# A four-layer hybrid trunk on one core: VectorE in traced order at the layer norms, six slots for split weights, the mixers' residual scaled at out_proj

## The chip, the cores and the metric

The kernel is one program on one core of a Trainium2 chip. The metric is device time in microseconds (us) of that core. The kernel before took 2769.28 us, the median of three runs between 2768.69 and 2770.76. The engines are TensorE (PE; its weight loads are PEld), VectorE (DVE), ScalarE (ACT), GpSimd (POOL) and SyncE (SP), which issues most of the transfers. An engine takes its instructions strictly in the order in which the program lists them, and an instruction whose input is not there holds up all that stand behind it on that engine.

## The reference

The kernel computes a decoder trunk of four layers on one sequence of 512 tokens with 1024 channels, all in float32. The mixers are Gated DeltaNet (GDN), HGRN2, GLA and GDN again. Each is followed by a dense SwiGLU channel mixer, and each of the eight branches ends in a residual and a layer norm:

```python
for i in range(DEPTH):                       # DEPTH = 4
    m = (gated_deltanet, hgrn2, gla)[i % 3](x, ...)      # each ends in  o @ w_out
    x = layer_norm(DN_ALPHA * x + m, mix_ln_g[i], mix_ln_b[i])
    x = layer_norm(DN_ALPHA * x + swiglu(x, ffn_w_in[i], ffn_w_down[i]), ffn_ln_g[i], ffn_ln_b[i])
return x

def layer_norm(x, g, b):
    mu = mean(x, -1); var = mean(square(x - mu), -1)
    return (x - mu) * rsqrt(var + LN_EPS) * g + b

def swiglu(x, w_in, w_down):
    gate, up = split(x @ w_in, 2)
    return (silu(gate) * up) @ w_down
```

## The kernel before

**Products.** Every float32 product is three matmuls: each operand is split into a high and a low part, and high by low, high by high and low by high are summed (mm3, L176 to L178). The activations live transposed in SBUF as xTh and xTl, with channels on the partitions and tokens along the rows. A weight block of 1 MB or less is loaded by SP, ACT copies it to a rounded high part (whi, L142), and DVE subtracts to get the low part (wlo, L144). These pairs live in the pool "wsplit", which has four slots for high and four for low parts. A fifth pair waits until PE has used the first for the last time.

**The norms.** out_proj and the FFN's second product end in down_norm. The 512 tokens are four tiles of 128. The last half of the output channels is done tile by tile from eight blocks of resident weights, called res, some of which stand in wsplit slots: down(i) on PE, 24 matmuls, then norm(i). norm(i) adds the residual (add_x, L331), takes the statistics (bn_stats L361, bn_aggr L364), works out the inverse root by ten instructions on one column (L365 to L377), and then ACT normalises the tile in two halves of 512 channels (L382; for the last tile's first half DVE does it, L380). PE then transposes the tile (tr(i): put_xT, L214, eight transposes into two PSUM tiles xtp). For each half the four 128-channel pieces get the norm's scale and bias on their way out of PSUM: pieces 0 and 2 by ACT (L224), 1 and 3 by DVE (L222), all into one tile xt. Then ACT copies the half to xTh (L226) and DVE subtracts to get xTl (L227).

**The order around a norm.** The next phase's first four weight slices, w0 to w3, are fed in between: begin() multiplies them with token columns 0 to 255 (tiles 0 and 1) first, and 256 to 511 afterwards. The traced order on PE is down(0), down(1), down(2) with tr(0) inside, down(3) with tr(1) inside, w0, tr(2), w1, tr(3), w2, w3, and then the other columns. Before GLA and GDN, w0 is a narrow slice of 16 matmuls (L190). manual_schedule holds PE to this order. The other engines get theirs from the framework's scheduler, which places each instruction by its estimate of when it can run. There are seven such norms, after four mixers and three FFNs. The last FFN writes the output and has no next phase.

**The residual.** x itself, needed again one branch later, also gets scale and bias, on POOL: affine(), two instructions per half tile (L390, L394), 16 in all, held back by a dependency until the last x^T is written. After an FFN's norm each half tile is then stored to DRAM (store, L385), and the next mixer loads it again in get_x (L236), when out_proj begins.

**The starts of the next mixers.** After an FFN's norm HGRN begins with forget gates and products on DVE (L1011, L1012, L901 to L917), GLA with a gate on ACT and DVE (L1074 to L1088), and GDN with a chain of small gate columns on DVE (gcols, L573 to L588), which PE needs at L590. At the mixers' end, finish() works out an inverse root over the heads (occ and rsq, L511 to L516, L133 to L137), DVE and POOL scale the heads by it (on, L519), and PE transposes them (ytp, L528) for out_proj.

Of the kernel before, what the change touches and what calls it, by code (L numbers as in the profile page):

```python
# [13 lines left out]
ALU = mybir.AluOpType  # L14
# [3 lines left out]
P = 128  # L18
T = 512
D = 1024  # L20
NT = T // P
# [16 lines left out]
class Net:  # L38
    def __init__(self, ctx, tc, a, out):
        self.tc, self.nc, self.a, self.out = tc, tc.nc, a, out  # L40
        pool = lambda name, bufs, **kw: ctx.enter_context(tc.tile_pool(name=name, bufs=bufs, **kw))
        self.cp = pool("const", 1)
        self.raw = pool("raw", 2)
        self.wsp = pool("wsplit", 4)
        self.xp = pool("xT", 1)
        self.ar = pool("arena", 1)
        self.col = pool("cols", 2)
        self.mid = pool("mid", 1)
        self.dr = pool("dram", 2, space=bass.MemoryType.DRAM)
        self.acc = pool("acc", 4, space=PSUM)  # L50
        self.mx = pool("mx", 4, space=PSUM)
        self.n = 0
        self.deferred, self.late, self.lmask = [], [], None
        self.lo_eng = self.nc.vector
        self.xT = tuple(self.xp.tile([P, KD, T], F32R, name=n) for n in ("xTh", "xTl"))
        self.consts()
# [172 lines left out]

    def get_x(self):  # L230

        x = []
        for i in range(NT):
            x.append([self.t2("st", s="x") for _ in range(2)])
            for e in range(2):
                self.nc.sync.dma_start(x[i][e], self.x_dram[i * P:(i + 1) * P, e * 512:(e + 1) * 512])  # L236
        return x

    def early(self, unit):
# [94 lines left out]
    def down_norm(self, kt, w, k0, pools, alpha, g, b, to_dram, to_out, rtags):  # L334

        nc, V = self.nc, self.nc.vector
        n = len(kt)
        lnw = []
        for v in (g, b):
            for e in range(2):  # L340
                t = self.t2("vz", s="lnw")
                nc.gpsimd.dma_start(t, v[e * 512:(e + 1) * 512].partition_broadcast(P))
                lnw.append(t)
        if not to_out:
            gb = self.columns(self.rows([v.rearrange("(k p) -> k p", p=P) for v in (g, b)]), "lngb")
        stats = self.small([P, NT, 2, 6], s="bnst")
        self.down_part(kt, w, k0, 0, pools[0], alpha)
        for i in range(NT):
            V.bn_stats(stats[:, i, 0], self.x[i][0])
        ps = [self.bank(pools[1], [P, 512], "dn") for _ in range(NT)]  # L350
        kr = n - self.NRES
        for k, wt in self.kblocks(w, 1, k0, k0 + kr):
            for i in range(NT):
                self.mm_tok(ps[i], i, kt[k - k0], wt, k == k0, False)
        res = list(self.kblocks(w, 1, k0 + kr, k0 + n, rtags))
        next(self.nxt)
        if to_dram:
            self.x_dram = self.dr.tile([T, D], F32, tag="xd", name=self.nm("xd"))

        def norm(i):  # L360
            V.bn_stats(stats[:, i, 1], self.add_x(ps[i], i, 1, alpha))  # L361
            c = self.small([P, 6], s="lnc", bufs=4)
            mean, var, vh, rstd, z, shift = (c[:, k:k + 1] for k in range(6))
            V.bn_aggr(c[:, 0:2], stats[:, i])  # L364
            V.tensor_scalar(vh, var, LN_EPS, -0.5, ALU.add, ALU.mult)  # L365
            V.tensor_scalar(rstd.bitcast(I32), vh.bitcast(I32), -0.5, RSQRT_MAGIC - float(0x40400000), ALU.mult, ALU.add)
            for _ in range(3):
                V.scalar_tensor_tensor(z, rstd, vh, rstd, ALU.mult, ALU.mult)
                V.scalar_tensor_tensor(rstd, z, 1.5, rstd, ALU.add, ALU.mult)
            x = self.x[i]  # L370
            if to_out:
                for e in range(2):
                    V.scalar_tensor_tensor(x[e], x[e], mean, lnw[e], ALU.subtract, ALU.mult)
                    V.scalar_tensor_tensor(x[e], x[e], rstd, lnw[2 + e], ALU.mult, ALU.add)
                    store(i, e, self.out[0])
                return
            V.scalar_tensor_tensor(shift, mean, -1.0, rstd, ALU.mult, ALU.mult)  # L377
            for e in range(2):
                if i == NT - 1 and e == 0:
                    V.tensor_scalar(x[e], x[e], mean, rstd, ALU.subtract, ALU.mult)  # L380
                else:
                    nc.scalar.activation(x[e], x[e], AF.Identity, bias=shift, scale=rstd)  # L382

        def store(i, e, dst):
            nc.sync.dma_start(dst[i * P:(i + 1) * P, e * 512:(e + 1) * 512], self.x[i][e])  # L385

        def affine(i):
            for e in range(2):
                r = self.x[i][e]
                first = nc.gpsimd.tensor_tensor(r, r, lnw[e], ALU.mult)  # L390
                if i == 0:
                    self.tc.add_manual_dep(first.ins, self.xT_done.name, mybir.DependencyInfo(
                        mybir.DependencyClass.Sync, mybir.DependencyReason.DATA), reason="x^T first")
                nc.gpsimd.tensor_tensor(r, r, lnw[2 + e], ALU.add)  # L394
                if to_dram:
                    store(i, e, self.x_dram)

        def down(i, k1, k2):
            for k, wt in res[k1:k2]:
                self.mm_tok(ps[i], i, kt[k - k0], wt, k == k0, k == k0 + n - 1)  # L400

        def tr(i):
            for e in range(2):
                self.put_xT(i, self.x[i][e], e, gb)

        with self.tc.manual_schedule(engines={mybir.EngineType.PE}):
            for i in range(NT):
                cut = 0 if to_out or i < 2 else i - 1
                down(i, 0, cut)
                if cut:  # L410
                    tr(i - 2)
                down(i, cut, None)
                norm(i)
            if not to_out:
                next(self.nxt)
                tr(2)
                next(self.nxt)
                tr(3)
                next(self.nxt)
        if not to_out:  # L420
            with self.tc.manual_schedule(engines={mybir.EngineType.Pool}):
                for i in range(NT):
                    affine(i)
# [358 lines left out]
    def solve(self, nt):  # L782

        nc = self.nc
        V, S, G, mm = nc.vector, nc.scalar, nc.gpsimd, nc.tensor.matmul
# [19 lines left out]
            V.tensor_tensor(pr[:, :, :c, :c], u8[:, :, :c, :c], m8[:, :, c:c + 1, :c].broadcast_to([P, 2, c, c]), ALU.mult)  # L805
            V.tensor_reduce(u8[:, :, :c, c], pr[:, :, :c, :c], AX.X, ALU.add)
        pr = sv((P, 8, 8, 8), "pr8")
        z = self.small([P, 8, 8], s="z8", bufs=1)
        V.tensor_tensor(pr, U[:, 0:8, None, 0:8].broadcast_to([P, 8, 8, 8]),
                        M[:, None, 8:16, 0:8].broadcast_to([P, 8, 8, 8]), ALU.mult)  # L810
        V.tensor_reduce(z, pr, AX.X, ALU.add)
# [375 lines left out]
```

## Time and profile before

| what | value |
|---|---|
| median of three runs | 2769.28 us |
| the profiled execution's own time | 2768.41 us |
| its span, first to last instruction | 2766.5 us |
| mean granted TensorE clock, of full speed | 0.986 |
| PE / PEld busy | 97% / 81% |
| DVE / ACT / POOL busy | 55% / 38% / 11% |

The profiled execution lies within the three runs. About 1.9 us of its time lie outside the span. PE's busy share is an upper bound, since the ends of pipelined matmuls are modelled; what is certain are the stretches in which PE did nothing, and the profile names for each the instruction that ended it. The granted clock is 1.0 at 2.4 GHz and 0.5 at 1.2 GHz.

### The profile page before, as it was taken

The page shows a single profiled execution, that of the slowest core. Times are in us where ns is not written, and L with a number is a line of the kernel's source. Part 1 is how long each engine was busy: PE and PEld are TensorE (multiplying, and loading weights), DVE is VectorE, ACT ScalarE, POOL GpSimd, SP SyncE. Part 2 cuts the span into 40 slices and gives each one's busy share as a digit, 9 for nine tenths or more (in the row PEclk, how much of TensorE's full clock was granted, in tenths as well). Part 3 has the DMA queues.
Part 4 walks back from the last instruction along what each step waited for, and adds up shares of the span by engine and source line. Part 5 has one row for each costly group of instructions (what it writes and reads, how often), then busy time and mean ns, then how long its engine had stood idle before and what let it go on. Part 6 is the DMA issues. An engine that isn't in the chain of part 4 may idle for free.

```text
span 2766.5 us, 37874 instructions
## 1 busy us (share of the span) xinstructions
PE 2672.5 (97%) x15279; PEld 2235.3 (81%) x15279; DVE 1512.6 (55%) x3015; ACT 1061.0 (38%) x2107; POOL 304.2 (11%) x316
## 2 busy tenths in 40 slices
PE   9999999999899999999999999999979999999998
PEld 8787888888777778888887888888877787888886
DVE  6667753333777776323366665333378576733335
ACT  5464542222444444222244644222235455422221
POOL 1111040001300004000030004000031111210000
PEclk9999999999999999999999999999989999999999
DMA  4213233233221232232322232232322132232222
GB/s 140 62 47 100 85 95 104 92 98 115 74 77 50 85 115 92 92 107 92 108 75 81 77 122 92 93 105 91 110 74 77 47 100 77 69 117 96 92 99 69
DMA packets 198719, 248.29 MB, mean 90 GB/s; under 512 B 8890, under 2 KB 152384, under 8 KB 198544
## 3 DMA queue, kind: packets, MB, share of 16 engines
q1 hardware_dynamic: 195152, 237.29, 26.8%
q0 software_dynamic: 3392, 8.59, 1.0%
q8 instruction: 120, 1.97, 0.3%
q14 instruction: 55, 0.45, 0.1%
HBM read 237.47 MB, written 8.39 MB: 89 GB/s over the span
## 4 chain that ended last, share of the span: by engine, by line
PE 82%; DVE 12%; issue 2%; ACT 2%; POOL 0%; DMA 0%; SPq 0%; DVEq 0%; ACTq 0%; POOLq 0%
PE pj L177 16%; PE pj L178 16%; PE pj L176 16%; PE dn L176 8%; PE dn L178 8%; PE dn L177 7%; DVE wlo L144 2%; DVE am L898 2%; DVE qk L616 1%; PE sc L931 1%; PE tp L491 1%; PE vp L177 1%; PE xtp L214 1%; PE vp L176 1%; PE kk L672 1%
## 5 line engine op out<-in xcount | busy, mean ns | idle before, releaser
L176 PE MATMUL pj<-xTl,whi 128*128 128x512 f32 (+1 forms) x2472 | 927.3, 375 | 0.0
L177 PE MATMUL pj<-xTh,whi 128*128 128x512 f32 (+1 forms) x2472 | 926.3, 375 | 0.0
L178 PE MATMUL pj<-xTh,wlo 128*128 128x512 f32 (+1 forms) x2472 | 925.4, 374 | 0.0
L144 DVE TENSOR_TENSOR wlo<-wraw,whi 128x1024 fp32r<-128x1024 f32 x400 | 509.9, 1277 | 688.7 <-ACT whi L142 682.9
L142 ACT CAST whi<-wraw 128x1024 fp32r<-128x1024 f32 x400 | 419.8, 1051 | 1160.6 <-PE pj L177 656.3
L177 PEld LDWEIGHTS pj<-xTh,whi 128*128 128x128 f32 x2472 | 470.8, 190 | 78.0 <-issue 0.7
L176 PEld LDWEIGHTS pj<-xTl,whi 128*128 128x128 f32 x2472 | 470.7, 190 | 78.0 <-issue 0.7
L178 PEld LDWEIGHTS pj<-xTh,wlo 128*128 128x128 f32 x2472 | 470.6, 190 | 77.8 <-issue 0.5
L440 DVE TENSOR_TENSOR sg<-sg,pj 128x512 f32<-128x512 f32 x88 | 60.4, 686 | 240.2 <-PE pj L178 240.2
L176 PE MATMUL dn<-wlo,hhi 128*128 128x512 f32 x416 | 161.8, 389 | 0.0
L177 PE MATMUL dn<-whi,hhi 128*128 128x512 f32 x416 | 161.8, 389 | 0.0
L178 PE MATMUL dn<-whi,hlo 128*128 128x512 f32 x416 | 161.8, 389 | 0.0
L390 POOL TENSOR_TENSOR x<-x,lnw 128x512 f32<-128x512 f32 x56 | 83.5, 1491 | 312.1 <-issue 243.9
L331 DVE SCALAR_TENSOR_TENSOR x<-x,dn 128x512 f32<-128x512 f32 x96 | 64.9, 685 | 61.2 <-PE dn L178 61.0
L394 POOL TENSOR_TENSOR x<-x,lnw 128x512 f32<-128x512 f32 x56 | 90.9, 1623 | 4.2
L177 PEld LDWEIGHTS dn<-whi,hhi 128*128 128x128 f32 x416 | 78.1, 188 | 16.3
L178 PEld LDWEIGHTS dn<-whi,hlo 128*128 128x128 f32 x416 | 78.1, 188 | 16.2
L176 PEld LDWEIGHTS dn<-wlo,hhi 128*128 128x128 f32 x416 | 78.1, 188 | 16.2
L176 PE MATMUL dn<-wlo,nt 128*128 128x512 f32 x224 | 87.5, 390 | 0.0
L178 PE MATMUL dn<-whi,nt 128*128 128x512 f32 x224 | 87.1, 389 | 0.0
L177 PE MATMUL dn<-whi,nt 128*128 128x512 f32 x224 | 87.1, 389 | 0.0
L176 PE MATMUL dn<-wlo,xTh 128*128 128x512 f32 x192 | 76.6, 399 | 0.0
(386 smaller groups left out, 3471.8 us busy)
## 6 DMA issues: line engine op xcount, KB each, us to landing
wraw<-in_ffn_w_in SPq DMA_DIRECT2D x88, 1024.0 KB, 5.1
wraw<-in_ffn_w_down SPq DMA_DIRECT2D x40, 1024.0 KB, 5.0
wraw<-in_gdn_w_in SPq DMA_DIRECT2D x32, 1024.0 KB, 5.8
wraw<-in_hgrn_w_in SPq DMA_DIRECT2D x16, 1024.0 KB, 5.7
wraw<-in_gla_w_in SPq DMA_DIRECT2D x12, 1024.0 KB, 5.3
wraw<-in_gdn_w_out SPq DMA_DIRECT2D x8, 1024.0 KB, 5.0
xd<-x SPq DMA_DIRECT2D x24, 256.0 KB, 2.0
x<-xd SPq DMA_DIRECT2D x24, 256.0 KB, 6.1
```

Source lines behind the costliest of these rows:

```text
L142: nc.scalar.copy(hi, raw)
L144: (eng or nc.vector).tensor_tensor(lo, raw, hi.bitcast(F32), ALU.subtract)
L176: mm(out, ah, bl, start=start, stop=False)
L177: mm(out, ah, bh, start=False, stop=False)
L178: mm(out, al, bh, start=False, stop=stop)
L214: nc.tensor.transpose(ps[:, k], src[:, k * P:(k + 1) * P], self.ident)
L331: self.nc.vector.scalar_tensor_tensor(s, s, alpha, ps, ALU.mult, ALU.add)
L390: first = nc.gpsimd.tensor_tensor(r, r, lnw[e], ALU.mult)
L394: nc.gpsimd.tensor_tensor(r, r, lnw[2 + e], ALU.add)
L440: nc.vector.tensor_tensor(s, s, pss[2 + j], ALU.mult)
L491: self.nc.tensor.transpose(ps[:, i], src[:, i * P:(i + 1) * P], self.ident)
L898: V.copy_predicated(av[:, c, js], self.lmask[b][:, gs], pm[:, c, gs])
```

## The change

There are three edits. DVE joins PE in the manual schedule of down_norm, so that within it DVE runs in the order in which the code is traced. The pool wsplit gets six slots instead of four; to make room, a small tile z8 of the GDN solve shares a buffer with its products, and the scratch of POOL's transfers shrinks to 1024. And the residual after an FFN's norm is stored as soon as it is normalised, without scale and bias; get_x of the next mixer loads the scale and bias again (lnp, four transfers from POOL's queue, into the three-slot buffer "tr") and POOL applies them there, 16 instructions again (L242, L243). The order of x in get_x is now first halves, then second halves. The POOL instructions after the mixers' own norms stay. Lines of the changed kernel lie 7 higher from add_x on and 9 higher after down_norm.

```diff
-        self.wsp = pool("wsplit", 4)
+        self.wsp = pool("wsplit", 6)
...
     def get_x(self):
-        x = []
-        for i in range(NT):
-            x.append([self.t2("st", s="x") for _ in range(2)])
-            for e in range(2):
+        G = self.nc.gpsimd
+        x = [[self.t2("st", s="x") for _ in range(2)] for _ in range(NT)]
+        for e in range(2):
+            if self.x_gb:
+                gb = [self.t2("tr", s="lnp") for _ in range(2)]
+                for t, v in zip(gb, self.x_gb):
+                    G.dma_start(t, v[e * 512:(e + 1) * 512].partition_broadcast(P))
+            for i in range(NT):
                 self.nc.sync.dma_start(x[i][e], self.x_dram[i * P:(i + 1) * P, e * 512:(e + 1) * 512])
+                if self.x_gb:
+                    G.tensor_tensor(x[i][e], x[i][e], gb[0], ALU.mult)
+                    G.tensor_tensor(x[i][e], x[i][e], gb[1], ALU.add)
         return x
...
                     nc.scalar.activation(x[e], x[e], AF.Identity, bias=shift, scale=rstd)
+                if to_dram:
+                    store(i, e, self.x_dram)
...
                 nc.gpsimd.tensor_tensor(r, r, lnw[2 + e], ALU.add)
-                if to_dram:
-                    store(i, e, self.x_dram)
...
-        with self.tc.manual_schedule(engines={mybir.EngineType.PE}):
+        with self.tc.manual_schedule(engines={mybir.EngineType.PE, mybir.EngineType.DVE}):
...
-        if not to_out:
+        if to_dram:
+            self.x_gb = g, b
+        elif not to_out:
             with self.tc.manual_schedule(engines={mybir.EngineType.Pool}):
...
-        z = self.small([P, 8, 8], s="z8", bufs=1)
+        z = self.small([P, 8, 8], tag="prd", s="z8", bufs=2)
...
-    nc = bacc.Bacc("TRN2", target_bir_lowering=False, num_devices=1)
+    nc = bacc.Bacc("TRN2", target_bir_lowering=False, num_devices=1, dynamic_dma_scratch_size=1024)
```

The first place is DVE at the norm of layer 0's mixer, from the inverse root of tile 2 to the residual of tile 3. lnc_619 are the columns of tile 2, xt_621 and xt_623 the two halves of tile 1's x^T, and the add on dn_591 belongs to tile 3. Before:

```order
L222 TENSOR_SCALAR xt_621_3600<-xtp_620_3595,lngb_566_3224 128x128
L368 SCALAR_TENSOR_TENSOR lnc_619_3576<-lnc_619_3576 128x1
L222 TENSOR_SCALAR xt_623_3612<-xtp_622_3607,lngb_566_3224 128x128
L369 SCALAR_TENSOR_TENSOR lnc_619_3576<-lnc_619_3576 128x1
L222 TENSOR_SCALAR xt_621_3600<-xtp_620_3595,lngb_566_3224 128x128
L368 SCALAR_TENSOR_TENSOR lnc_619_3576<-lnc_619_3576 128x1
L222 TENSOR_SCALAR xt_623_3612<-xtp_622_3607,lngb_566_3224 128x128
L369 SCALAR_TENSOR_TENSOR lnc_619_3576<-lnc_619_3576 128x1
L377 SCALAR_TENSOR_TENSOR lnc_619_3576<-lnc_619_3576 128x1
L227 TENSOR_TENSOR xTl_85<-xt_621_3600,xTh_84 128x4x128
L227 TENSOR_TENSOR xTl_85<-xt_623_3612,xTh_84 128x4x128
L331 SCALAR_TENSOR_TENSOR x_559_3208<-x_559_3208,dn_591_3400 128x512
```

And now (wlo_643 and wlo_646 are the fifth and sixth weight pair of the FFN that follows):

```order
L375 SCALAR_TENSOR_TENSOR lnc_619_3576<-lnc_619_3576 128x1
L144 TENSOR_TENSOR wlo_643_3932<-wraw_641_3928,whi_642_3930 128x1024
L376 SCALAR_TENSOR_TENSOR lnc_619_3576<-lnc_619_3576 128x1
L384 SCALAR_TENSOR_TENSOR lnc_619_3576<-lnc_619_3576 128x1
L222 TENSOR_SCALAR xt_621_3600<-xtp_620_3595,lngb_566_3224 128x128
L144 TENSOR_TENSOR wlo_646_3961<-wraw_641_3928,whi_645_3959 128x1024
L222 TENSOR_SCALAR xt_621_3600<-xtp_620_3595,lngb_566_3224 128x128
L227 TENSOR_TENSOR xTl_85<-xt_621_3600,xTh_84 128x4x128
L222 TENSOR_SCALAR xt_623_3612<-xtp_622_3607,lngb_566_3224 128x128 x2
L227 TENSOR_TENSOR xTl_85<-xt_623_3612,xTh_84 128x4x128
L338 SCALAR_TENSOR_TENSOR x_559_3202<-x_559_3202,dn_591_3400 128x512
```

The two halves of tile 1's x^T no longer alternate with each other and with the inverse root of tile 2. The whole inverse root now stands ahead of them, two weight splits stand among them, and one half follows the other. The same holds at all seven norms.

The second place is ACT at the same norm. x_556 and x_557 are the two halves of tile 2, xt_621 and xt_623 again tile 1. Before:

```order
L224 ACTIVATE xt_621_3600<-xtp_620_3595,lngb_566_3224 128x128
L224 ACTIVATE xt_623_3612<-xtp_622_3607,lngb_566_3224 128x128
L224 ACTIVATE xt_621_3600<-xtp_620_3595,lngb_566_3224 128x128
L224 ACTIVATE xt_623_3612<-xtp_622_3607,lngb_566_3224 128x128
L226 CAST xTh_84<-xt_621_3600 128x4x128
L226 CAST xTh_84<-xt_623_3612 128x4x128
L382 ACTIVATE x_556_3203<-x_556_3203,lnc_619_3576 128x512
L142 CAST whi_609_3438<-wraw_608_3436 128x1024
L142 CAST whi_611_3442<-wraw_608_3436 128x1024
L382 ACTIVATE x_557_3204<-x_557_3204,lnc_619_3576 128x512
```

And now:

```order
L224 ACTIVATE xt_621_3600<-xtp_620_3595,lngb_566_3224 128x128
L226 CAST xTh_84<-xt_618_3546 128x4x128
L224 ACTIVATE xt_623_3612<-xtp_622_3607,lngb_566_3224 128x128
L142 CAST whi_642_3930<-wraw_641_3928 128x1024
L142 CAST whi_645_3959<-wraw_641_3928 128x1024
L389 ACTIVATE x_556_3199<-x_556_3199,lnc_619_3576 128x512
L389 ACTIVATE x_557_3200<-x_557_3200,lnc_619_3576 128x512
L224 ACTIVATE xt_621_3600<-xtp_620_3595,lngb_566_3224 128x128
L226 CAST xTh_84<-xt_621_3600 128x4x128
L224 ACTIVATE xt_623_3612<-xtp_622_3607,lngb_566_3224 128x128
L226 CAST xTh_84<-xt_623_3612 128x4x128
```

The normalisation of tile 2 now stands ahead of the second piece of tile 1, and the weight copies split there are the pair after w0 to w3. Those two copies write over slots of res, and wait for the last matmuls of down(3).

The third place is POOL at the end of the HGRN mixer, where x_1366 and its like are the residual, lnp the scale and bias, and on_1349 the last head. Before:

```order
L342 DMA lnw_1377_8807<-in_mix_ln_b 128x512
L474 DMA stage_1685_11208<-in_ffn_ln_g 8x128
L474 DMA stage_1685_11208<-in_ffn_ln_b 8x128
L519 TENSOR_TENSOR on_1349_8718<-on_1349_8718,occ_1364_8769 128x512
L390 TENSOR_TENSOR x_1366_8785<-x_1366_8785,lnw_1374_8801 128x512
```

And now, from the second of the new instructions on:

```order
L483 DMA stage_1689_11213<-in_ffn_ln_g 8x128
L243 TENSOR_TENSOR x_1366_8766<-x_1366_8766,lnp_1375_8775 128x512
L242 TENSOR_TENSOR x_1368_8768<-x_1368_8768,lnp_1374_8774 128x512
L242 TENSOR_TENSOR x_1370_8770<-x_1370_8770,lnp_1374_8774 128x512
L243 TENSOR_TENSOR x_1368_8768<-x_1368_8768,lnp_1375_8775 128x512
L243 TENSOR_TENSOR x_1370_8770<-x_1370_8770,lnp_1375_8775 128x512
L242 TENSOR_TENSOR x_1372_8772<-x_1372_8772,lnp_1374_8774 128x512
L242 TENSOR_TENSOR x_1367_8767<-x_1367_8767,lnp_1376_8790 128x512
L243 TENSOR_TENSOR x_1372_8772<-x_1372_8772,lnp_1375_8775 128x512
L238 DMA lnp_1377_8791<-in_ffn_ln_b 128x512
L242 TENSOR_TENSOR x_1369_8769<-x_1369_8769,lnp_1376_8790 128x512
L242 TENSOR_TENSOR x_1371_8771<-x_1371_8771,lnp_1376_8790 128x512
```

One more scaling and a transfer follow, and then the head. The head's scaling, which stood behind transfers alone, now has eleven of the sixteen residual instructions between itself and the transfer of the FFN's norm weights.

## Rows read from the trace of the kernel before

**Rows 1.** Page, section 1: busy us, share of the span, instructions.

```profile
PE 2672.5 (97%) x15279; PEld 2235.3 (81%) x15279; DVE 1512.6 (55%) x3015; ACT 1061.0 (38%) x2107; POOL 304.2 (11%) x316
```

**Rows 2.** Waits of PE, whole span: us in total, times, longest us.

```profile
PE tp L491 <- DVE qk L916: 18.1, 4, 10.6
PE xtp L214 <- DVE x L380: 13.1, 7, 2.4
PE pg L590 <- DVE gcols L588: 12.1, 2, 11.8
```

**Rows 3.** Waits of PE, start of GLA: us in total, times, longest us.

```profile
PE tp L491 <- DVE qk L916: 4.7, 1, 4.7
...
PE pz L1082 <- DVE gk L1075: 1.7, 1, 1.7
```

**Rows 4.** Timeline of PE, norm of layer 0's mixer: start, us, instruction, [idle before].

```profile
346.27 1.04 PE L214 MATMUL xtp<-ident,x 128*128 128x128 f32 x8
...
351.27 0.28 PE L176 MATMUL pj<-xTl,whi 128*128 128x256 f32 x1
...
359.70 1.09 PE L214 MATMUL xtp<-ident,x 128*128 128x128 f32 x8 [1.66 <-DVE x L380]
```

**Rows 5.** Timeline of DVE, same norm.

```profile
333.32 0.69 DVE L331 SCALAR_TENSOR_TENSOR x<-x,dn 128x512 f32<-128x512 f32 x1 [1.18 <-PE dn L178]
...
336.74 0.16 DVE L377 SCALAR_TENSOR_TENSOR lnc<-lnc 128x1 f32<-128x1 f32 x1
...
352.07 2.35 DVE L144 TENSOR_TENSOR wlo<-wraw,whi 128x1024 fp32r<-128x1024 f32 x2
...
360.88 1.84 DVE L222 TENSOR_SCALAR xt<-xtp,lngb 128x128 f32<-128x128 f32 x4 [1.24 <-ACT xt L224]
362.92 1.29 DVE L227 TENSOR_TENSOR xTl<-xt,xTh 128x512 fp32r<-128x512 f32 x2 [0.19 <-ACT xTh L226]
```

**Rows 6.** Timeline of ACT, same norm.

```profile
336.94 1.52 ACT L382 ACTIVATE x<-x,lnc 128x512 f32<-128x512 f32 x2 [7.77 <-DVE lnc L377]
...
350.65 1.99 ACT L142 CAST whi<-wraw 128x1024 fp32r<-128x1024 f32 x2
...
354.78 1.83 ACT L224 ACTIVATE xt<-xtp,lngb 128x128 f32<-128x128 f32 x4 [1.43 <-PE xtp L214]
356.65 1.14 ACT L226 CAST xTh<-xt 128x512 fp32r<-128x512 f32 x2
```

**Rows 7.** Windows: us, PE, PEld, DVE, ACT, POOL busy, PEclk, DMA share, GB/s.

```profile
755.90:759.80 3.90, 3.66 (x11) 3.09 (x12) 3.38 (x8) 2.16 (x5) 0.00 (x0) 0.50 0.78 192
1456.20:1459.60 3.40, 3.21 (x10) 2.72 (x11) 2.36 (x6) 3.39 (x6) 0.00 (x0) 0.50 0.63 218
2072.40:2077.50 5.10, 5.10 (x24) 4.79 (x25) 2.32 (x5) 1.04 (x4) 0.00 (x0) 0.51 0.35 90
```

**Rows 8.** Timeline of DVE, first and last gate columns, layers 0 and 3.

```profile
28.97 0.19 DVE L574 SCALAR_TENSOR_TENSOR gcols<-gcols 128x32 f32<-128x32 f32 x1
...
33.59 0.19 DVE L588 SCALAR_TENSOR_TENSOR gcols<-gcols,par 128x32 f32<-128x32 f32 x1
...
2055.74 1.16 DVE L574 SCALAR_TENSOR_TENSOR gcols<-gcols 128x32 f32<-128x32 f32 x1
...
2072.04 0.19 DVE L588 SCALAR_TENSOR_TENSOR gcols<-gcols,par 128x32 f32<-128x32 f32 x1
```

**Rows 9.** Timeline of SP's queue, start of HGRN.

```profile
733.55 22.33 SPq L385 DMA_DIRECT2D xd<-x  x8
```

**Rows 10.** Page, section 5: POOL's scaling; busy us, mean ns.

```profile
L390 POOL TENSOR_TENSOR x<-x,lnw 128x512 f32<-128x512 f32 x56 | 83.5, 1491 | 312.1 <-issue 243.9
```

**Rows 11.** Timeline of DVE, end of HGRN.

```profile
1003.93 0.16 DVE L511 TENSOR_SCALAR occ<-oss 128x8 f32<-128x8 f32 x1
```

**Rows 12.** Timeline of POOL, end of HGRN.

```profile
1007.43 1.45 POOL L519 TENSOR_TENSOR on<-on,occ 128x512 f32<-128x512 f32 x1 [5.24 <-DVE occ L516]
```

**Rows 13.** Timeline of PE, end of HGRN.

```profile
1017.94 1.03 PE L528 MATMUL ytp<-ident,on 128*128 128x128 f32 x8
```

More of the change, by code (lines that the diff above doesn't have):

```diff
@@ L52, in __init__ @@
         self.n = 0
-        self.deferred, self.late, self.lmask = [], [], None
+        self.deferred, self.late, self.lmask, self.x_gb = [], [], None, None
         self.lo_eng = self.nc.vector
```

## The prediction

> **What bounds the kernel now.** Read the busy shares first: PE is busy for 97% of the span, DVE for 55% [rows 1]. So the kernel is PE's own work plus the moments in which PE has nothing to do, and a change to the other engines can only move those moments, 94 us in all (the span of 2766.5 less 2672.5). The second view is the list of PE's waits. Three entries concern this change [rows 2, 3]. At the seven norms PE waits for DVE's half of the last tile's normalisation, 13.1 us together, 1.66 five times and 2.4 before GLA and GDN. At the start of HGRN it waits 10.6 us for DVE's product qk, and at GLA's 4.7 us for the same, with 1.7 us for the gate gk before. At the start of the last GDN it waits 11.8 us for the gate columns. The third view is the timelines of PE, DVE, ACT and POOL at a norm and at the starts. The reader is to see that PE passes the norm almost without a gap: the first slice of the next phase starts at 351.27, directly behind the last tile's products, and the one wait is 1.66 us, just ahead of 359.70 [rows 4].
>
> **The norms: what the traced order costs.** All times are on the axis of the kernel before. A matmul of the resident half takes 0.23 us: between 346.27 and 351.27 stand eight transposes (0.8) and 18 such matmuls. A tile of 24 is 5.5 us. Undisturbed, a norm lasts from add_x at 333.32 to the end of L377 at 336.90, 3.58 us [rows 5]. ACT's two normalisations take 1.52 us, a scaled piece 0.46 us on either engine, the copy of a half 0.57 and its subtraction 0.65 [rows 5, 6].
>
> In the new order the four pieces of a half write one tile and wait for each other in turn: ACT, DVE, ACT, DVE, copy, subtraction. Before, the two halves alternated, so one engine worked on one half while the other did the second: the last tile's pieces and copies lie between 354.78 or 360.88 and 3.3 to 3.9 us later. Now a half takes 0.46 × 3 + 0.57 + 0.65 = 2.6 us after its first piece, and the second half follows on the first.
>
> - norm(1) on DVE: 338.8 (5.5 after 333.3) to 342.4.
> - x^T of tile 0: DVE's first piece may only follow here. ACT has tile 1's two normalisations ahead of the next piece (to 343.9), so the first half ends at 346.1, the second at 348.75.
> - PE: the second half of tr(1) needs a PSUM tile that this second half gives back at 347.45. Its first half is through at 346.7. That is 0.8 us of waiting, and down(3) ends at 352.05, not 351.27.
> - norm(2) on DVE: 348.75, plus 3.58, plus one wlo of 1.2 us (half of 2.35, [rows 5]) that now stands inside: 353.6. ACT's two copies of the next weights, 1.0 each [rows 6], wait for down(3) and end at 353.1, so they hold up nothing more.
> - x^T of tile 1: ACT normalises tile 2 first, to 355.2. Then piece 0.46, piece 0.46, copy 0.57, subtraction 0.65, with the hops: 357.45. The second wlo lies beside ACT's work. The second half: 360.1.
>
> PE's first slice needs tile 1. It starts at 357.45, 5.4 us after down(3). Its first 12 matmuls (0.12 each, half the columns) end at 358.9, and the second half is there at 360.1: 1.2 us more. norm(3) then starts at 360.1 and with the last half tile is out by 364.3, with tr(3) due at 365.3: the old wait of 1.66 is gone. Tile 3's x^T is ready at 372.2 and 374.5 while PE reaches it at 371.9; PE's order there now takes first halves of other slices in between, and I put 0.8 on it. The sum for one norm: 0.8 + 5.4 + 1.2 + 0.8 = 8.2, instead of 1.66. Before GLA and GDN the first slice is 16 matmuls instead of 24 and covers less; I take 9.4 instead of 2.4. Five times 6.6 and twice 7.0 make **47 us more**. The lower bound is the case in which the first slice starts in time: all 13.1 us go. The upper one is 54: if the order in the columns 256 to 511 doesn't help, PE waits 0.3 and then 1.5 us there instead of 0.8.
>
> **The clock.** The row shows that the 4.71 us wait at GLA was followed by 3.4 us at 0.50 of the granted clock, 1.2 GHz, with PE busy [rows 7]. A wait of 5.4 us should do the same: 3.4 us at half speed lose 1.7 us. But the slower first slice also uses up the 1.2 us wait in its middle, so I add 0.5 per norm, **4 us** (0 to 12). The Trainium skill, page "TensorE: Matmul & The Clock Gate", section "HAM oscillation — how this bites in real kernels", says that each wait long enough drops the clock, and that the throttled time costs half of itself. The rows agree; taken bare, that rule would make it 1.7 × 7 = 12 us.
>
> **The starts: what leaves.** POOL's 16 instructions last 1.49 us on average [rows 10] and run beside the first DVE work of the next mixer. There DVE is stretched. The gate columns of layer 3, beside POOL, take 2055.74 to 2072.23, 16.5 us; the same rows in layer 0, with POOL idle, 28.97 to 33.78, 4.8 us [rows 8]. The difference of 11.7 is the wait of 11.8. At HGRN I leave 1 us of 10.6, since the chain from the gate to qk has to be walked in any case. At GLA gk stands on POOL behind the residual, and that wait goes; of 4.7 I leave 0.2. The waits give back 11.7 + 9.6 + 6.2 = 27.5. Behind them PE worked at half clock for 3.66, 3.21 and 5.10 us [rows 7], half of which, 6.0, returns as well. Together **33.5 us less**; the ends are 0, if something else is as late there, and 36 with the stores below. What is late next is HGRN's qk itself. The eight stores of x leave SP earlier: its queue stood for 22.33 us at them [rows 9], with weight loads behind. That is hidden or gives 2 us.
>
> **The mixers' ends: what comes.** Of 16 new POOL instructions at the end of HGRN, eleven stand between a transfer of norm weights and the last head's scaling. That transfer waits for PE and goes out at about 1001.5; before, POOL stood idle from 1002.19 on, 5.24 us, behind it and its fellow [rows 12]. 11 × 1.49 = 16.4, with two transfers some 17.5, so the head is scaled from 1019 to 1020.5 instead of 1007.43 to 1008.9. PE transposes it at 1017.94 [rows 13]: 2 to 3 us of waiting, where 9 us had covered it. DVE's inverse root at 1003.93 [rows 11] runs beside POOL now and is stretched as the gate columns were, 3.4-fold: 3.4 us become 11.5, still ahead of POOL. At GLA and at the last GDN the same cover holds. I take **3 us**, between 0 and, if each of the three ends lost a third of what the starts give back, 27. The page "SBUF — State Buffer", section "Who interferes with whom", states that a DVE instruction with two SBUF inputs waits for the whole of a POOL instruction that reads SBUF. The gate columns of [rows 8] agree. By it the move takes the blocking along to out_proj, a rival below.
>
> The lnp transfers take the buffer "tr" in its pauses; z8 and the smaller scratch add no instruction: nothing, at most 1 us either way. The six slots bring splits forward, but PE waits for none of them in [rows 2].
>
> **The sum.** 2768.4 (the profiled execution, 0.9 below the median) + 47 + 4 − 33.5 + 3 = 2788.9, and with the 0.9: **2790 us**, 0.7% slower. Its own range, with 15 us less or 16 more, is 2775 to 2806.
>
> **The rivals.**
> - *The norm hides its order.* If DVE comes to tile 1 earlier than I walked it, say because ACT runs ahead, PE starts its slice in time, and the waits of 13.1 partly go as well: 2769.3 − 33.5 + 3 − 4 = 2735. Against it stands that the pieces are bound by semaphores in the new order. For it: a walk by hand adds up durations that could overlap. 0.18.
> - *The norm costs half of it* (+28 with the clock), and the edits cancel: 2769.3 + 28 − 33.5 + 3 = 2767. What decides is how far ACT's normalisation of tile 2 lies beside DVE's splits. 0.09.
> - *The starts don't recover.* Behind POOL the next late thing is ACT or a weight split, and the 33.5 stay: 2769.3 + 47 + 4 + 3 = 2823. Layer 0 speaks against it for GDN, nothing does for HGRN. It decides once ACT's part of the chain is as long as DVE's. 0.08.
> - *The blocking moves along.* At three mixers' ends PE loses some 9 us each, as much as it gained at the starts: 2790 − 3 + 27 = 2814. The 9 us of cover at the head speak against it. 0.07.
> - My forecast: 0.58.
>
> Two runs of this kernel can be told apart from about 0.2%, 5.5 us. Faster than that: the first rival and 0.03 of the second, 0.21. Within it: the second's other 0.06 and 0.04 of the forecast's lower edge, 0.10. Slower: the rest, 0.69. The range runs from 2738 to 2820; the first rival's better part and the third stay outside.
>
> **What would show it.** In the profile of the changed kernel: PE waiting 5 to 6 us ahead of pj L176 on DVE xTl L227, seven times, about 35 to 45 us in the list of waits, and no xtp on x of the last tile. The two wlo between L375 and L376 on DVE. No wait at pg, and at most 1 to 2 us for qk at HGRN. POOL idle at the starts, and busy from about 1001 at the end of HGRN, with on at about 1019. The forecast is wrong if the first slice after down(3) starts within 2 us, or if the waits at qk and gcols keep their length.

## The result and the profile after

The changed kernel takes 2804.25 us (median of four runs, 2802.40 to 2808.99) against 2768.99 for the kernel before on the same chip: ratio 1.0129, 95% interval 1.0112 to 1.0147. It is slower, as forecast, by 35 us where 21 had been predicted. Its profiled execution took 2808.99 us, the slowest of the four; its span of 2807.3 is 40.8 above that of before, at a mean granted clock of 0.978 instead of 0.986. All sums below are made in these two spans.

The page's first section after, with the columns of [rows 1]:

```profile
PE 2694.5 (96%) x15279; PEld 2249.2 (80%) x15279; DVE 1524.1 (54%) x3015; ACT 1062.2 (38%) x2107; POOL 320.1 (11%) x328
```

PE's idle time has grown from 94 to 113 us only. The other 22 us are busy time: the same 15279 instructions, more of them at half clock. The list of PE's waits says where the idle time moved; it answers to [rows 2]:

```profile
PE pj L176 <- DVE xTl L227: 25.5, 6, 5.0
PE pj L190 <- DVE xTl L227: 13.2, 5, 5.1
...
PE ob L978 <- DVE Sst L974: 6.1, 2, 5.1
...
PE tp L500 <- DVE qk L925: 4.3, 4, 1.4
...
PE xtp L214 <- DVE xt L222: 3.7, 7, 0.6
PE dn L176 <- ACT xTh L463: 2.8, 1, 2.8
...
PE pg L599 <- DVE gcols L597: 0.2, 1, 0.2
```

The first slice's wait for tile 1 is new: 36.6 us at the seven norms, in the two entries for xTl. The wait for the last tile's normalisation, 13.1 us in [rows 2], is gone. The longest wait for qk is 1.4 us instead of 10.6, and that for the gate columns 0.2 instead of 11.8. The entries for Sst and xTh are new too, and stand at the ends of GLA and HGRN.

PE at the norm of layer 0's mixer, to be laid beside [rows 4]:

```profile
347.99 0.66 PE L214 MATMUL xtp<-ident,x 128*128 128x128 f32 x4 [0.50 <-DVE xt L222]
...
352.38 0.39 PE L178 MATMUL dn<-whi,xTl 128*128 128x512 f32 x1
357.80 0.58 PE L176 MATMUL pj<-xTl,whi 128*128 128x256 f32 x1 [5.03 <-DVE xTl L227]
...
363.09 1.03 PE L214 MATMUL xtp<-ident,x 128*128 128x128 f32 x8
```

DVE there (to [rows 5]):

```profile
349.23 0.68 DVE L338 SCALAR_TENSOR_TENSOR x<-x,dn 128x512 f32<-128x512 f32 x1
...
352.53 1.22 DVE L144 TENSOR_TENSOR wlo<-wraw,whi 128x1024 fp32r<-128x1024 f32 x1
353.68 0.15 DVE L376 SCALAR_TENSOR_TENSOR lnc<-lnc 128x1 f32<-128x1 f32 x1
...
354.26 1.21 DVE L144 TENSOR_TENSOR wlo<-wraw,whi 128x1024 fp32r<-128x1024 f32 x1
355.95 0.41 DVE L222 TENSOR_SCALAR xt<-xtp,lngb 128x128 f32<-128x128 f32 x1 [0.48 <-ACT xt L224]
357.05 0.69 DVE L227 TENSOR_TENSOR xTl<-xt,xTh 128x512 fp32r<-128x512 f32 x1 [0.68 <-ACT xTh L226]
```

The walk of the prediction stands in the trace: tile 2's norm from 349.23 (predicted 348.75) with a wlo inside, and tile 1's first half ready for PE at 357.80 (357.45). Behind the wait PE runs at half clock. Two of the windows, with the columns of [rows 7], the first at this norm and the second at GLA's end:

```profile
356.10:362.90 6.80, 5.10 (x23) 5.11 (x24) 4.66 (x13) 1.69 (x3) 0.00 (x0) 0.50 0.46 154
...
1643.00:1649.80 6.80, 4.34 (x17) 3.69 (x17) 4.66 (x8) 2.15 (x10) 6.78 (x6) 0.50 0.34 106
```

The stretches at half clock come to 125 us in the whole span, 77 before. Those at the seven norms together, which begin while PE still waits:

```profile
sum 47.60, PE 33.19 PEld 32.00 DVE 31.86 ACT 15.72 POOL 0.00; mean PE 4.74 PEld 4.57 DVE 4.55 ACT 2.25 POOL 0.00
```

DVE's waits for ACT at the norm of layer 0's mixer (339 to 368 us after, then 338 to 361 before, where none is for xTl):

```profile
DVE xt L222 <- ACT xt L224: 4.2, 5, 1.6
DVE xTl L227 <- ACT xTh L226: 3.4, 5, 0.7
```

```profile
DVE xt L222 <- ACT xt L224: 1.2, 1, 1.2
```

**The account.** From the first transpose of a norm to its last, the seven norms lasted 21.0 to 21.7 us each before and 26.9 to 28.4 after: together +43.7. From the last transpose of a norm to the first ytp of the next mixer (HGRN, GLA, the last GDN) it is −11.2, −5.5 and −12.0: −28.7. From the second-last group of head transposes (ytp) to the norm, which is what a mixer's end stands for below, it is +10.8 at HGRN (43.0 us before) and +8.5 at GLA (49.0), and +4.2 in the last half of the last GDN (from its first ytp to the norm): +23.5. The rest is +2.3. The sum is 40.8.

HGRN's end, DVE, POOL and PE in turn (to [rows 11 to 13]):

```profile
1010.36 1.15 DVE L520 TENSOR_SCALAR occ<-oss 128x8 f32<-128x8 f32 x1 [1.27 <-ACT junk L508]
...
1017.78 4.30 DVE L136 SCALAR_TENSOR_TENSOR rsq<-rsq,occ 128x8 f32<-128x8 f32 x1
...
1022.92 0.17 DVE L525 TENSOR_SCALAR occ<-occ 128x8 f32<-128x8 f32 x1
```

```profile
1018.27 3.77 POOL L242 TENSOR_TENSOR x<-x,lnp 128x512 f32<-128x512 f32 x3
...
1023.25 1.47 POOL L528 TENSOR_TENSOR on<-on,occ 128x512 f32<-128x512 f32 x1 [0.70 <-DVE occ L525]
```

```profile
1023.88 0.66 PE L537 MATMUL ytp<-ident,on 128*128 128x128 f32 x4 [0.56 <-DVE on L528]
...
1029.39 0.79 PE L176 MATMUL dn<-wlo,xTh 128*128 128x512 f32 x1 [2.81 <-ACT xTh L463]
```

An instruction of 0.17 us lasts 4.30 us, until three of POOL's have ended. And GLA's end, DVE before, then DVE and PE after:

```profile
1615.15 3.69 DVE L455 TENSOR_TENSOR xTl<-y,xTh 128x512 fp32r<-128x512 f32 x6
```

```profile
1634.05 10.17 DVE L464 TENSOR_TENSOR xTl<-y,xTh 128x512 fp32r<-128x512 f32 x6
1644.14 0.28 DVE L974 COPY Sst<-su 128x128 f32<-128x128 f32 x1
```

```profile
1644.48 0.79 PE L978 MATMUL ob<-Sst,qk 128*128 128x128 f32 x2 [5.07 <-DVE Sst L974]
```

The six subtractions took 3.69 us before and take 10.17 now. The copy of the state (Sst) stands behind them, and PE waits 5.07 us for it.

### The profile page after: what moved, and what is told of

Its sections match the earlier page's. It is cut to its first block, busy times and chain, and to the rows that moved or that the text cites. A ratio compares the mean times of both kernels' runs of the same rounds, so it can differ in the third digit from the quotient of the medians.

```text
span 2807.3 us, 37793 instructions
## 1 busy us (share of the span) xinstructions
PE 2694.5 (96%) x15279; PEld 2249.2 (80%) x15279; DVE 1524.1 (54%) x3015; ACT 1062.2 (38%) x2107; POOL 320.1 (11%) x328
## 4 chain that ended last, share of the span: by engine, by line
PE 80%; DVE 13%; ACT 5%; issue 2%; DMA 0%; SPq 0%; DVEq 0%; ACTq 0%
PE pj L176 16%; PE pj L177 16%; PE pj L178 16%; PE dn L176 7%; PE dn L178 7%; PE dn L177 7%; DVE wlo L144 2%; DVE am L907 2%; DVE qk L625 1%; PE sc L940 1%; ACT whi L142 1%; ACT x L389 1%; PE tp L500 1%; PE vp L178 1%; PE vp L176 1%
## 5 line engine op out<-in xcount | busy, mean ns | idle before, releaser
L224 ACT ACTIVATE xt<-xtp,lngb 128x128 f32<-128x128 f32 x112 | 49.6, 454 | 73.6 <-PE xtp L214 37.9
L177 PE MATMUL dn<-whi,xTh 128*128 128x512 f32 x192 | 77.3, 402 | 0.0
```

The source lines that it names most:

```text
L177: mm(out, ah, bh, start=False, stop=False)
L224: nc.scalar.activation(t[:, k], ps[:, k], AF.Identity, scale=fg, bias=fb)
```

## The experiments

Ratios are to the kernel before on the same chip, with 95% intervals.

**One part at a time.** The first four kernels split the change.

```diff
# the change without VectorE in the manual schedule
-        with self.tc.manual_schedule(engines={mybir.EngineType.PE, mybir.EngineType.DVE}):
+        with self.tc.manual_schedule(engines={mybir.EngineType.PE}):
```

> The changed kernel with one edit undone: DVE is no longer in the manual schedule of down_norm, so its order at the norms is the scheduler's again; six slots and the moved residual stay. Theory (the traced order of DVE costs about 6.2 us at each of seven norms, the moved residual gives 29 at the starts and takes 23 at the mixers' ends): 2769 - 29 + 23 = 2763 us, PE's waits on xTl L227 gone, one wait of about 1.7 us per norm on the last tile's x as before, POOL still busy at the mixers' ends. Rival (the mixers' ends lose because the norms shifted DVE's and ACT's work): the ends are as before and the time is about 2741. Rival (six slots hide the weight splits at the norms): the waits on the last tile's x are gone too, 13 us less, about 2750.

Measured: 2755.29, ratio 0.9953 (0.9936 to 0.9969). The norms are back at 21.0 to 21.1 us, the starts keep −34, and the ends keep their loss: HGRN +13.1, GLA +8.3. The last half of the last GDN loses 1.0 only. PE waits 12.1 us for the last tile's x again, so both rivals fall.

```diff
# the kernel before, with VectorE in traced order and nothing else
-        with self.tc.manual_schedule(engines={mybir.EngineType.PE}):
+        with self.tc.manual_schedule(engines={mybir.EngineType.PE, mybir.EngineType.DVE}):
```

> The kernel before with one edit alone: DVE joins PE in the manual schedule of down_norm; four slots, residual as before. Theory: the seven norms lose what they lose in the changed kernel, some 44 us, and the starts and ends are as before: about 2813 us, with PE waiting about 5 us on xTl L227 at each norm. Rival (the loss comes from the fifth and sixth weight pair that six slots bring into the norm of tile 2): clearly less, under 2795.

Measured: 2822.00, ratio 1.0189 (1.0174 to 1.0205). PE's waits:

```profile
PE pj L176 <- DVE xTl L227: 25.4, 5, 5.1
PE tp L491 <- DVE qk L916: 19.5, 4, 10.3
PE pg L590 <- DVE gcols L588: 15.1, 2, 14.8
PE pj L190 <- DVE xTl L227: 13.3, 5, 5.1
```

The traced order alone brings the two entries for xTl, as in the changed kernel, and leaves those of the starts. Of the 56 us by which its profiled span exceeds that of before, 45.3 lie at the seven norms and 6.8 at the start of the last GDN.

```diff
# the kernel before, with the new get_x and the early store and nothing else
...
-        if not to_out:
+        if to_dram:
+            self.x_gb = g, b
+        elif not to_out:
```

> The kernel before with one edit alone: the residual after an FFN's norm takes scale and bias at out_proj; four slots, DVE's order free. Theory: starts 29 less, mixers' ends 23 more, about 2763 us; no wait at pg of the last GDN, and waits of several us on ob and dn at the ends of HGRN and GLA. Rival (the ends lose only with six slots or with DVE's traced order): about 2741.

Measured: 2759.32, ratio 0.9962 (0.9949 to 0.9975). The ends lose here too, HGRN +9.3, GLA +9.5 and the last half of the last GDN +8.1, so the rival falls.

```diff
# the kernel before, with six slots, the shared z8 and the smaller scratch
-        self.wsp = pool("wsplit", 4)
+        self.wsp = pool("wsplit", 6)
```

> The kernel before with one edit alone: six slots for split weights (with z8 sharing a buffer and the smaller transfer scratch that make room). Theory: PE waits for no weight split, and the two splits still fall into the last tile's norm, so nothing moves: 2769 within 3 us. Rival: the splits leave the norm of the last tile and the waits there go, 13 us less, about 2756.

Measured: 2769.02, ratio 0.9996 (0.9986 to 1.0005), with the waits of before. So the traced order is +52 alone and +49 on top of the others (2804.25 against 2755.29), the residual −11, the slots nothing; whether the slots give a few us beside the residual (2755.29 against 2759.32) the intervals leave open.

**What the ends lose by.** In the first of these kernels the end of HGRN shows the mechanism bare. DVE, then POOL:

```profile
988.51 10.61 DVE L281 TENSOR_TENSOR wr<-wraw,wr 128x512 fp32r<-128x512 f32 x1
...
1005.67 0.16 DVE L520 TENSOR_SCALAR occ<-oss 128x8 f32<-128x8 f32 x1
```

```profile
988.55 1.31 POOL L243 TENSOR_TENSOR x<-x,lnp 128x512 f32<-128x512 f32 x1
...
997.28 1.28 POOL L243 TENSOR_TENSOR x<-x,lnp 128x512 f32<-128x512 f32 x1
998.51 0.59 POOL L238 DMA_DIRECT2D lnp<-in_ffn_ln_b  x1
```

The rows of POOL left out are six more of these instructions, back to back. A subtraction that takes 0.68 us elsewhere ends when POOL's run of eight instructions has ended and its transfer is issued. The next kernel takes these instructions away, and the four transfers of scale and bias with them.

```diff
# with VectorE free; the scale and bias at out_proj left out
-                    G.dma_start(t, v[e * 512:(e + 1) * 512].partition_broadcast(P))
...
-                    G.tensor_tensor(x[i][e], x[i][e], gb[0], ALU.mult)
-                    G.tensor_tensor(x[i][e], x[i][e], gb[1], ALU.add)
```

> This is the changed kernel with VectorE left to the scheduler again, and with the scale and bias of the residual at out_proj left out entirely: the 16 GpSimd instructions per mixer and the four lnp transfers are gone, so what it computes differs from the reference in this part alone. Theory 1: at the mixers' ends it is these 16 instructions, running beside VectorE's inverse root and state copies, that cost the 22 us which the ends lost in the version with VectorE free (HGRN +13, GLA +8.4, GDN +1). Then the ends return to the kernel before (HGRN from 56 us to 43) while the starts keep their gain, and the time is 2755 - 22 = 2733, between 2728 and 2738. Rival: the ends lost through the new order of the x transfers and of the other engines there, not through GpSimd's work; then the time stays at 2755 (2750 to 2760), and the stretch at HGRN's end keeps some 56 us.

Measured: 2735.09, ratio 0.9873 (0.9859 to 0.9888): theory 1 holds. HGRN's end falls from 56.1 to 43.4 us (43.0 before), GLA's from 57.3 to 49.2 (49.0). The last half of the last GDN stays as it was with VectorE free (+1.1 to before). DVE's inverse root at HGRN's end:

```profile
992.17 0.17 DVE L512 TENSOR_SCALAR occ<-oss 128x8 f32<-128x8 f32 x1 [0.46 <-ACT junk L500]
...
994.39 0.17 DVE L517 TENSOR_SCALAR occ<-occ 128x8 f32<-128x8 f32 x1
```

The 20 us between this kernel and the first are the loss of these two ends, and it is POOL's work that makes it. The four transfers that left with it don't: the kernel with this work on VectorE, below, still has them, and HGRN's end takes 45.2 us there.

```diff
# with VectorE free; POOL's 16 instructions wait for the last head's scaling
+                        self.tc.add_manual_dep(r.ins, self.last_on.name, ...)
```

> The changed kernel with VectorE left to the scheduler, and with the 16 residual instructions on GpSimd held behind the last head's scaling (on), so that they start when the inverse root is done. Theory 1 (GpSimd stretches VectorE's inverse root at the ends): the ends recover most of their loss, HGRN's and GLA's ends come within 3 us of the kernel before, and the time is 2755 - 18 = 2737 (2732 to 2745). Rival A: the cost only moves, since the 16 instructions of about 1.5 us, 24 us in all, now end later and either run beside the norm or let add_x wait for the residual: 2755 (2750 to 2762), with a new wait of PE behind x. Rival B (it is the transfers or their order): also 2755, but with HGRN's end as long as in the version with VectorE free, about 56 us.

Measured: 2770.98, ratio 1.0004 (0.9995 to 1.0014): theory 1 of this run fails, by more than rival A gave. The inverse root is quick now, but what DVE does next is held instead. The list of PE's waits, the row of DVE at HGRN's end, and POOL's beside it:

```profile
PE dn L178 <- DVE xTl L466: 19.7, 4, 9.6
```

```profile
1009.80 12.16 DVE L466 TENSOR_TENSOR xTl<-y,xTh 128x512 fp32r<-128x512 f32 x2
```

```profile
998.02 13.01 POOL L243 TENSOR_TENSOR x<-x,lnp 128x512 f32<-128x512 f32 x8
...
1011.60 9.82 POOL L243 TENSOR_TENSOR x<-x,lnp 128x512 f32<-128x512 f32 x8
```

HGRN's end stays at 56.2 us and GLA's grows to 61.1. Neither of the two places tried at the end is free for 24 us of POOL.

**What the norms lose by.** Two kernels change the traced order, with the whole change and VectorE held to it.

```diff
# the two halves of a tile's x^T traced in turn
-            for e in range(2):
-                self.put_xT(i, self.x[i][e], e, gb)
+            self.put_xT2(i, self.x[i], gb)   # pieces of both halves alternate, then 2 copies, 2 subtractions
```

> The whole change, VectorE in traced order included, but with the two halves of a tile's x^T traced in turn: eight transposes, then the pieces of both halves alternating, then two copies and two subtractions. Theory: of the 6.2 us that a norm lost, the one half after the other accounts for about 2.6 us; the first slice still waits for tile 1, about 3 to 4 us instead of 5.0, since the inverse root of tile 2 and the two splits still stand ahead of it. 2804 - 7 x 2.6 = 2786 (2778 to 2795). Rival: the inverse root and the splits alone set the wait, and the halves cost nothing: 2804 (2798 to 2809), waits of PE for xTl unchanged near 38.7 us.

Measured: 2788.01, ratio 1.0062 (1.0047 to 1.0077), as the theory has it. At the norms the waits for xTl fall from 36.6 to 27.3 us, and each norm lasts 24.8 to 25.7 us.

```diff
# as that, and norm(2) traced behind tile 1's x^T
+                if not to_out and i == 3:
+                    norm(2)
                 down(i, cut, None)
-                norm(i)
+                if to_out or i != 2:
+                    norm(i)
```

> As the kernel with the halves in turn, VectorE in traced order too, but with norm(2) traced after the x^T of tile 1 instead of ahead of it. Theory: what cost 49 us is where norm(2) stands in the traced order, not that VectorE is held to an order. Then PE's first slice waits at most 1 us for tile 1, the list of waits has under 8 us of pj behind xTl, tile 2 is normalised late instead, with a cover of one or two slices, and the time is 2757 (2750 to 2768), that of the version with VectorE free. Rival: holding VectorE to any traced order costs, since splits stand fixed in the middle: 2775 or more. Second rival: the wait moves from tile 1 to tile 2 and 3, with PE waiting for x of the last tile 3 to 5 us per norm: 2780.

Measured: 2777.91, ratio 1.0028 (1.0019 to 1.0038). The theory fails. The number fits both rivals, the trace the second: the wait for tile 1 is gone, and PE waits for tile 2 instead, 22.0 us in seven waits. The one at layer 0:

```profile
359.43 1.61 PE L237 MATMUL xtp<-ident,x 128*128 128x128 f32 x8 [2.83 <-ACT x L413]
```

What the scheduler's order has and the traced ones lack is seen in the windows of 16 us from the norm's first transpose on, with the columns of [rows 7], for the kernel before, the changed one, and the one with norm(2) later:

```profile
339.24:355.24 16.00, 16.00 (x96) 14.13 (x95) 14.05 (x41) 11.21 (x20) 0.00 (x0) 1.00 0.00 0
```

```profile
339.86:355.86 16.00, 12.41 (x62) 9.95 (x60) 11.25 (x33) 9.26 (x15) 0.00 (x0) 1.00 0.00 1
```

```profile
341.54:357.54 16.00, 15.06 (x86) 12.98 (x84) 12.67 (x34) 9.29 (x16) 0.00 (x0) 1.00 0.01 1
```

DVE does 14.05 us of work in 16 before, and 11.25 and 12.67 in the traced orders. At a norm DVE is itself nearly full: each hop to ACT in which it stands still is lost, and the scheduler had filled the hops of x^T with the columns of the next inverse root. These two kernels give back 26 of the 49 us. That the other 23 are lost in such hops is argued from the windows and from DVE's waits for ACT; no run shows it by itself.

**The work on VectorE.** What remains is to give the residual's scale and bias to an engine that doesn't hold up another.

```diff
# with VectorE free; the 16 instructions on VectorE, traced just ahead of add_x
-                    G.tensor_tensor(x[i][e], x[i][e], gb[0], ALU.mult)
-                    G.tensor_tensor(x[i][e], x[i][e], gb[1], ALU.add)
+    def fix_x(self, e):                    # called before the add_x of each half
...
+                for t, op in zip(gb, (ALU.mult, ALU.add)):
+                    self.nc.vector.tensor_tensor(self.x[i][e], self.x[i][e], t, op)
```

> VectorE left to the scheduler, the residual stored without scale and bias, and the 16 instructions of scale and bias at out_proj given to VectorE instead of GpSimd, placed by the scheduler. A subtraction of the same shape on VectorE takes 0.65 us, so they are 10.4 us of VectorE per mixer, where GpSimd needed 24 us. Theory (GpSimd beside VectorE is what stretches the ends, not the additional work): HGRN's end falls from 56 us to 43 to 48, since eight of the 16 stand inside the inverse root and add 3 to 5 us there; 2735 without scale and bias at all plus 3 times 2 to 4 us makes 2743 (2736 to 2750). Rival: VectorE has no room for them at the ends, so the work costs its full 10 us per mixer: 2735 + 31 = 2766 or more.

Measured: 2738.50 (2737.69 to 2741.75), ratio 0.9892 (0.9877 to 0.9907), as the theory has it: faster than both kernels, and within 4 us of the one that leaves the work out. HGRN's end takes 45.2 us. DVE's inverse root and POOL's head there:

```profile
994.79 0.17 DVE L526 TENSOR_SCALAR occ<-oss 128x8 f32<-128x8 f32 x1
...
1002.79 0.16 DVE L531 TENSOR_SCALAR occ<-occ 128x8 f32<-128x8 f32 x1
```

```profile
1003.13 4.79 POOL L534 TENSOR_TENSOR on<-on,occ 128x512 f32<-128x512 f32 x1 [7.28 <-DVE occ L531]
```

The chain is stretched to 8 us by the instructions between its steps, and still PE comes to the first head at 1007.16 without a wait.

```diff
# as that, but held behind the last head's scaling
+                    self.tc.add_manual_dep(r.ins, self.last_on.name, ...)
```

> As the kernel with scale and bias on VectorE, but with the 16 instructions held behind the last head's scaling, so that they lie in the 9 to 10 us between that and PE's transposes of the head. Theory: the cover of 9 to 10 us takes the 10.4 us nearly whole, the ends are as short as without scale and bias, HGRN's 43 to 44 us, and the time is 2737 (2733 to 2743), faster than both kernels by over 1%. Rival: the 16 push the copies of the last heads (y, xTl) or the first add_x past their time, as the same hold on GpSimd did, where PE waited 19.7 us for xTl at the ends: 2750 to 2765, with new waits of dn behind xTl or x.

Measured: 2749.27, ratio 0.9929 (0.9912 to 0.9945), 11 us behind the unheld one: the theory fails. HGRN's end is the same, 45.5 us; GLA's is 52.9 instead of 49.2 and the last GDN's, from its last ytp group on, 30.3 instead of 25.3. At GDN, PE waits:

```profile
2332.46 0.50 PE L176 MATMUL dn<-nt,xTh 128*128 128x512 f32 x1 [1.93 <-DVE yy L553]
2358.93 1.33 PE L214 MATMUL xtp<-ident,x 128*128 128x128 f32 x5 [3.53 <-ACT x L397]
```

The work now lies directly ahead of the copies that PE waits for, and reaches into the norm. That is the rival in kind; the time lies 0.7 us below the 2750 to 2765 that it gave.

## Why the prediction was right, and where it was not

Direction and mechanism were right at the norms and the starts, and wrong at the mixers' ends. The time lay 14 us above the forecast, inside its own range. In the spans the forecast gave +20.5 and the trace +40.8, of which some 5 us are this execution alone. That the time stayed in the range is in part luck: the norms came out 7 us lower than forecast, and with the forecast's 51 there the time would have been some 2811, above the upper end of 2806.

- **The traced order at the norms.** Right in its steps: the start of the first slice was predicted to within 0.4 us, though the changed kernel comes to this norm 0.6 us later. The sum was 47, with the clock 51; measured 43.7 at the norms, and +49 to +52 for the order by itself. Inside it the shares were different, and two errors largely cancelled: the waits were too high by 20 us, the clock too low by 12.5. The waits are 36.6 and 3.7 for xt, less the old 13.1: 27.2 us. The 1.2 us in the middle of the first slice is 0.6 before GLA and the last GDN and nothing elsewhere, and the 0.8 at the last tiles doesn't appear: the first slice takes 5.3 us at half clock (357.80 to 363.09) instead of 2.9, and what follows is ready by then.
- **The clock.** Mis-sized: 4 us predicted, and 43.7 − 27.2 = 16.5 left over by the trace. I had taken 3.4 us at half clock per norm from [rows 7]; it was 6.8 at five norms, 10.2 at one and 3.4 at one. In these 47.6 us PE was busy for 33.2, and half of that is 16.6. The bare rule of the Trainium skill, page "TensorE: Matmul & The Clock Gate", section "HAM oscillation — how this bites in real kernels", by which the prediction estimated 12, was nearer than my allowance.
- **The starts.** −33.5 predicted, −28.7 measured in the changed kernel and −34 with VectorE free. The shortfall lies at GLA, −5.5 where the forecast's waits and clock made −7.8, and at the last GDN, −12.0 where they made −14.3. The gate columns of layer 3 now run from 2097.47 to 2103.49, 6.0 us instead of the 16.5 of [rows 8], and PE waits 0.2 us for them.
- **The mixers' ends.** This is the step that failed: "At GLA and at the last GDN the same cover holds. I take 3 us"; measured +23.5. At HGRN and GLA, 19.3 of it, POOL's work is shown to be the cause: with VectorE free the kernel without that work gets 12.8 and 8.1 us back. The +4.2 in the last GDN stay open: with VectorE free it is 1.0 with POOL's instructions and 1.1 without them. The rival that "the blocking moves along", held at 0.07, was right for two of the three ends. The stretch of the inverse root at HGRN was well seen (11.5 us predicted, 12.7 measured). Wrong was what I held against the cover: only POOL's scaling of the head. The inverse root itself began 4.9 us later after the ytp before it (994.6 to 1010.36, against 993.0 to 1003.93), behind stretched weight splits and ACT's sum of squares. And GLA's cover was that of the heads' scaling, while PE waits there for a copy of the state that stands behind six stretched subtractions. With these waits came stretches at half clock, 6.8 us at GLA.
- **The rivals.** "The norm hides its order" and "costs half of it" fell with the second kernel alone. "The starts don't recover" fell with the list of waits. The slots, put at nothing, measure nothing.

On the page "SBUF — State Buffer", section "Who interferes with whom", the Trainium skill says that a DVE instruction with two SBUF inputs contends with a POOL instruction that reads SBUF, and that the ports they share are an exclusive lock. The runs agree, and show it longer than one instruction of POOL: 10.61 us over eight.

## What to carry to other kernels

Work of GpSimd that reads SBUF isn't free because GpSimd is idle: price it as time taken from VectorE at the place where it runs, and ask at each place who waits for VectorE there. Before an engine is put into traced order, look at how full it is in that stage; one that is 55% busy on average was 88% busy at the norms (14.05 of 16 us), with two tiles' chains interleaved. When a chain on the critical path must lose its neighbour, giving 24 us of GpSimd to VectorE as 10 us can be cheaper than finding GpSimd another place.

## What the runs showed of the hardware that was not expected

VectorE doesn't always get in between two instructions of GpSimd: beside a run of eight, one subtraction of 0.68 us lasted 10.61, and two of them at another version's end 12.16, while at another place each small instruction lasted 1.15 to 1.22 us, about as long as one of GpSimd's. It goes the other way too: GpSimd's scaling of a head, 1.45 us in [rows 12], lasted 4.79 beside VectorE's subtractions. At five of the seven norms a wait of 5.0 to 5.1 us went with 6.8 us at half clock, which began 1.0 to 3.1 us before the wait ended, where [rows 7] had shown 3.4 beside one of 4.7.
